# A hybrid SSM and attention layer on one core: x, four weights and B once on the SP queue, small tables on GpSimd's, a written order for ScalarE and VectorE until hT is there, W units two projections later

## The chip, the core and the metric

The kernel runs on one core of a Trainium2 chip. The metric is the device time of one execution in microseconds: 744.75 us as the median of three runs (743.58 to 747.46) for the kernel before. One further execution was taken with the hardware profiler; everything said of engines, waits and single instructions comes from it.

## What is computed

One decoder layer with float32 inputs: x is 512 tokens by 1024 channels. Cut to what matters here:

```python
h = rms_norm(x, norm_w)
u, z_s, q, k, v, z_a, r_s, r_a = split(h @ w_in)          # 1024 -> 9216
# state space branch: 64 groups of 16 channels, 64 complex states each
dt = exp(log_dt); ab = exp(lam * dt)                      # complex
bb = (ab - 1) / lam * b
h_t = ab * h_(t-1) + bb u_t ;  y_t = Re(c h_t) + d_skip * u_t
g = gelu(y); y_s = (g * sigmoid(g @ w_glu) * silu(z_s)) @ w_ssm_out
# attention branch: three dilated windows, q and k normed and rotated
y_a = (dilated_attention(rope(norm(q)), rope(norm(k)), v) * silu(z_a)) @ w_attn_out
m = sigmoid(r_s) * y_s + sigmoid(r_a) * y_a
out = x + m @ w_o
```

## The kernel before

**Number format and units of work.** Every large matmul is done in three parts (`mm3`, L108 to L110): each operand is split into a rounded part "hi" and a remainder "lo", and hi·hi, hi·lo and lo·hi are summed. A projection (`cm_unit`) takes one weight block of 1024 by 128 and all of hT (h, transposed to channels on partitions) and is 24 matmuls of 512 columns; in the attention stage there are also projections by tokens (256 columns). A weight goes through a raw buffer `w_raw` (two of them), then `w_hi` on ScalarE (L93) and `w_lo` on VectorE (L95), three buffers each. `load_w` issues the DMA on the SP queue; `get_w` hands out the next weight of a fixed plan and issues loads up to two weights ahead.

**Stages in text order.** (1) ident, x (four tiles `x_t[r]` of 128 tokens), the inverse root of the mean square for two tiles at a time (L208 to L216, called h = 0 and 1), transposes into a PSUM bank `hps` (two channel blocks a bank), and from each bank `hT_hi` (ScalarE, L227) and `hT_lo` (VectorE, L228). (2) Eight projections give u, sent to DRAM and read back in another layout (`Uj`). The first three are computed in two halves of 256 columns. Between them stand the tables of the state space branch: `exp_exact`, `sincos`, the powers `pw` (L349 to L378), their transposes `AT` and `fT`, and `BB`, `BB2` (L423 to L428, in a tile `dd`). (3) For each of eight blocks j, `w_unit(j)` forms coefficients on VectorE and GpSimd (`coef`, L252 to L254, tile `ab`), transposes them on PE (L271, bank `wps`) and copies them to W; `x_unit(j)` multiplies by Uj (L282, bank `xps`) into Xs. (4) A scan along the sequence on VectorE (L610 to L612 and its neighbours, tile `scn`), while PE does further projections ("fillers" za, zs, v, rs, ra, from the list `order`) and `kps`. (5) The y units (L731, L733) with GELU, then the glu and output projections. (6) Attention in four head pairs; the ra projections not yet done lie in the last pair's stretch between scores and values (`ptp` transposes). (7) The last projections.

**What sets the order.** The text does not fix the order on an engine. A scheduler orders the instructions by their dependences and by its own estimate of when each can start; an explicit order exists where the text asks for it. So the mask steps (L497 to L510) stand early on VectorE though they are late in the text. DMAs were issued on SP's queue, except norm_w on ScalarE's. The fillers and `n_ra` (the count of ra projections in `order`; the other ones come after the head pairs) fix which weights follow which:

```python
order = [("za", c) for c in range(NP)] + [("zs", c) for c in range(KT)] + [("v0", 0), ("v", 0)]
order += [("rs", c) for c in range(KT)] + [("ra", c) for c in range(n_ra)]
...
for j in range(3, 8):
    u_unit(j)
    wx(*((), (), (0,), (1,), (2, 3))[j - 3])
...
for js in ((4,), (5, 6), (7, 8)):
    filler()
    wx(*js)
```

`wx(j)` issues `w_unit(j)` and then `x_unit(j - 1)`. During the loading of x, the weights' first two `w_lo` were given to GpSimd (`lo_w[0] = pool`).

Of the kernel before, what the change touches and what calls it, by code (L numbers as in the profile page):

```python
# [52 lines left out]
def tile_hybrid_block(ctx: ExitStack, tc: tile.TileContext, x, positions, norm_w, w_in, lam_re, lam_im,  # L53
# [3 lines left out]
    pe, act, dve, pool, sp = nc.tensor, nc.scalar, nc.vector, nc.gpsimd, nc.sync  # L57
# [55 lines left out]
    n_ra = 2  # L113
# [48 lines left out]
    def load_w(srcs, kts, cols):  # L162
        raw = wp.tile([P, kts, cols], F32, name="w_raw", tag="w_raw", bufs=2)
        w = cols // len(srcs)
        for i, s in enumerate(srcs):
            sp.dma_start(raw[:, :, i * w:(i + 1) * w], s.rearrange("(k p) c -> p k c", p=P))
# [20 lines left out]
    dve.tensor_copy(nwc, nps[:, 0:KT])  # L187
    x_all = big.tile([P, NB, D], F32, name="x_all", tag="s3")
# [16 lines left out]
    junk = big.tile([P, D], F32, name="junk", tag="s6a")  # L205
    for h in range(2):
        for r in (2 * h, 2 * h + 1):
            act.activation(junk, x_t[r], AF.Square, accum_out=ss[:, r:r + 1])  # L208
# [3 lines left out]
        for r in (2 * h, 2 * h + 1):  # L212
            if r % 2:
                act.activation(x_t[r], x_t[r], AF.Copy, scale=rst[:, r:r + 1])
            else:
                dve.tensor_scalar(x_t[r], x_t[r], rst[:, r:r + 1], None, op0=ALU.mult)  # L216
        for q in range(KT // 2):
# [6 lines left out]
            for k in range(2):  # L224
# [4 lines left out]
                                         op0=ALU.mult, op1=ALU.subtract)  # L229
    if "hT" in dbg:  # L230
# [64 lines left out]
    lr = scr([G, N])  # L295
    li = scr([G, N])
    dt = scr([G, 1])
    sp.dma_start(lr, lam_re[0])
    sp.dma_start(li, lam_im[0])
    sp.dma_start(dt, log_dt.rearrange("o g -> g o"))  # L300
# [36 lines left out]
    dte = scr([G, 1])  # L337
    exp_exact(dte, dt, [G, 1], "ea")
    mag = scr([G, N])
    th_ = scr([G, N])  # L340
    dve.tensor_scalar(th_, lr, dte, None, op0=ALU.mult)
    exp_exact(mag, th_, [G, N], "eb")
    dve.tensor_scalar(th_, li, dte, None, op0=ALU.mult)
    sn = scr([G, N])
    cs = scr([G, N])
    sincos(sn, cs, th_, [G, N], "la")

    pw = big.tile([G, 2, 9, N], F32, name="pw", tag="s7a")
    dve.tensor_tensor(pw[:, 0, 0], mag, cs, op=ALU.mult)  # L349
    dve.tensor_tensor(pw[:, 1, 0], mag, sn, op=ALU.mult)  # L350
    den = scr([G, N])
    nr = scr([G, N])
    t1 = scr([G, N])
    t2 = scr([G, N])
    dve.tensor_tensor(den, lr, lr, op=ALU.mult)
    dve.tensor_tensor(t1, li, li, op=ALU.mult)
    dve.tensor_tensor(den, den, t1, op=ALU.add)
    dve.reciprocal(den, den)
    dve.tensor_scalar(nr, pw[:, 0, 0], -1.0, None, op0=ALU.add)
    dve.tensor_tensor(t1, nr, lr, op=ALU.mult)  # L360
    dve.tensor_tensor(t2, pw[:, 1, 0], li, op=ALU.mult)
    dve.tensor_tensor(t1, t1, t2, op=ALU.add)
    dve.tensor_tensor(pw[:, 0, 8], t1, den, op=ALU.mult)
    dve.tensor_tensor(t1, pw[:, 1, 0], lr, op=ALU.mult)
    dve.tensor_tensor(t2, nr, li, op=ALU.mult)
    dve.tensor_tensor(t1, t1, t2, op=ALU.subtract)
# [289 lines left out]
    for js in ((4,), (5, 6), (7, 8)):  # L656
        filler()
        wx(*js)
# [436 lines left out]
```

## Time and profile before

| | |
|---|---|
| median of three runs | 744.75 us (743.58 to 747.46) |
| the profiled execution | 745.33 us, of which the span of its instructions is 743.5 us |
| mean granted TensorE clock | 0.983 |
| VectorE, ScalarE, GpSimd busy | 63%, 45%, 23% of the span |
| largest groups on ScalarE and VectorE | w_hi 105.9 us (100 of 1060 ns), w_lo 124.2 us (98 of 1268 ns) |
| DMA | 85.51 MB, mean 115 GB/s |

How to read the rows: PE is the matmul engine, PEld its weight loads, DVE VectorE, ACT ScalarE, POOL GpSimd, SP the engine that issues most DMAs. A row of the timeline has the start, the duration, the engine, the line in the kernel, the operation, the tile written, the tiles read, shape, count, and in brackets how long the engine was idle before it and what released it. A row of the list of waits has who waited for whom, the total, how often, and the longest. In a row of a group the count is followed by the busy time and the mean of one in ns, then the idle time ahead of it.

### The profile page before, as it was taken

What the parts mean: (1) busy time and instruction counts of PE and PEld (TensorE: products, weight loads), DVE (VectorE), ACT (ScalarE), POOL (GpSimd) and SP (SyncE); (2) the same over time, 40 slices, a digit from 0 to 9 for tenths busy, and PEclk for the clock granted to TensorE, in tenths of its full rate; (3) what the DMA queues carried; (4) which work ended last, traced back from release to release, by engine and by line L of the source; (5) the groups of instructions that cost most, each with busy time, mean ns of one, the idle gap of its engine ahead of it and who ended that gap; (6) DMA issues with size and microseconds to landing.
All of it is one profiled execution on the core that took longest, in us unless ns stands there. A gap on an engine that the chain in (4) does not pass through costs nothing.

```text
span 743.5 us, 13321 instructions
## 1 busy us (share of the span) xinstructions
PE 702.2 (94%) x5221; PEld 615.8 (83%) x5221; DVE 468.4 (63%) x958; ACT 336.7 (45%) x628; POOL 168.7 (23%) x304
## 2 busy tenths in 40 slices
PE   3699999999979688999999999999999999999998
PEld 2687788788857477888899999899999989778997
DVE  6768757989867454674336679667747654536631
ACT  6443544233388574433143475464446435433310
POOL 3345631110001001550001224142304311200000
PEclk9899999999999899999999999999999999999999
DMA  9754654674637765447324212213211321356321
GB/s 203 129 143 110 159 114 105 144 178 118 120 101 138 136 132 143 154 133 217 91 80 120 86 57 85 59 30 98 85 46 57 95 77 57 109 179 226 124 100 57
DMA packets 156014, 85.51 MB, mean 115 GB/s; under 512 B 40232, under 2 KB 148144, under 8 KB 155824
## 3 DMA queue, kind: packets, MB, share of 16 engines
q1 hardware_dynamic: 155936, 84.66, 44.1%
q8 instruction: 41, 0.67, 0.4%
q14 instruction: 21, 0.17, 0.1%
q10 hardware_dynamic: 16, 0.00, 0.0%
HBM read 73.18 MB, written 11.47 MB: 114 GB/s over the span
## 4 chain that ended last, share of the span: by engine, by line
PE 78%; DMA 8%; DVE 6%; SPq 3%; ACT 2%; issue 2%; POOL 0%; DVEq 0%; ACTq 0%
PE pj L110 21%; PE pj L109 21%; PE pj L108 21%; DMA w_raw<-in_w_in_dram 4%; PE ot L926 3%; PE ptp L940 2%; PE sps L870 2%; PE qtp L827 1%; DMA kd<-kt 1%; DVE w_lo L95 1%; PE xps L282 1%; DMA dd<-kd 1%; PE wps L271 1%; DMA gd<-th 1%; DVE scn L610 1%
## 5 line engine op out<-in xcount | busy, mean ns | idle before, releaser
L93 ACT ACTIVATE w_hi<-w_raw 128x1024 fp32r<-128x1024 f32 x100 | 105.9, 1060 | 200.6 <-PE pj L109 89.4
L95 DVE TENSOR_TENSOR w_lo<-w_raw,w_hi 128x1024 fp32r<-128x1024 f32 x98 | 124.2, 1268 | 64.1 <-ACT w_hi L93 62.9
L108 PE MATMUL pj<-hT_hi,w_hi 128*128 128x512 f32 (+1 forms) x344 | 135.0, 395 | 9.7 <-ACT w_hi L93 5.6
L109 PE MATMUL pj<-w_lo,hT_hi 128*128 128x256 f32 x512 | 144.0, 281 | 0.0
L110 PE MATMUL pj<-w_hi,hT_lo 128*128 128x256 f32 x512 | 143.9, 281 | 0.0
L108 PE MATMUL pj<-w_hi,hT_hi 128*128 128x256 f32 x512 | 143.8, 281 | 0.0
L109 PE MATMUL pj<-hT_lo,w_hi 128*128 128x512 f32 (+1 forms) x344 | 133.5, 389 | 0.4 <-DVE hT_lo L228 0.4
L110 PE MATMUL pj<-hT_hi,w_lo 128*128 128x512 f32 (+1 forms) x344 | 133.3, 388 | 0.1
L109 PEld LDWEIGHTS pj<-w_lo,hT_hi 128*128 128x128 f32 x512 | 96.2, 188 | 1.4 <-issue 0.7
L108 PEld LDWEIGHTS pj<-w_hi,hT_hi 128*128 128x128 f32 x512 | 96.0, 188 | 1.1 <-issue 0.9
L110 PEld LDWEIGHTS pj<-w_hi,hT_lo 128*128 128x128 f32 x512 | 96.0, 188 | 0.7
L108 PEld LDWEIGHTS pj<-hT_hi,w_hi 128*128 128x128 f32 x344 | 67.0, 196 | 23.1 <-ACT w_hi L93 5.8
L110 PEld LDWEIGHTS pj<-hT_hi,w_lo 128*128 128x128 f32 x344 | 66.5, 193 | 14.5 <-issue 0.8
L109 PEld LDWEIGHTS pj<-hT_lo,w_hi 128*128 128x128 f32 x344 | 66.8, 194 | 13.5 <-DVE hT_lo L228 0.8
L814 POOL TENSOR_TENSOR rt<-qraw,tC 128x256 f32<-128x256 f32 x12 | 16.5, 1371 | 127.0 <-DVE qraw L807 93.0
L109 PE MATMUL pj<-w_lo,mT_hi 128*128 128x256 f32 x128 | 36.2, 283 | 0.0
L110 PE MATMUL pj<-w_hi,mT_lo 128*128 128x256 f32 x128 | 36.2, 283 | 0.0
L108 PE MATMUL pj<-w_hi,mT_hi 128*128 128x256 f32 x128 | 36.2, 283 | 0.0
L849 ACT ACTIVATE Pt<-Pt,st 128x256 f32<-128x256 f32 (+1 forms) x64 | 31.0, 487 | 5.0 <-DVE st L847 4.8
L799 DVE TENSOR_REDUCE ssq<-qsq 128x8 f32<-128x512 f32 x24 | 16.4, 685 | 26.3 <-ACT qsq L798 26.2
L835 ACT ACTIVATE qkp<-qtp,wcol 128x512 fp32r<-128x512 f32 (+1 forms) x32 | 20.7, 685 | 20.7 <-PE qtp L827 15.6
L796 ACT COPY qraw<-pj 128x512 f32<-128x512 f32 x24 | 14.1, 586 | 35.0 <-PE pj L110 34.8
(272 smaller groups left out, 1368.5 us busy)
## 6 DMA issues: line engine op xcount, KB each, us to landing
w_raw<-in_w_in_dram SPq DMA_DIRECT2D x40, 512.0 KB
w_raw<-in_w_in_dram SPq DMA_DIRECT2D x64, 256.0 KB
dd<-kd SPq DMA_DIRECT2D x8, 512.0 KB
w_raw<-in_w_glu_dram SPq DMA_DIRECT2D x8, 512.0 KB
w_raw<-in_w_ssm_out_dram SPq DMA_DIRECT2D x8, 512.0 KB
w_raw<-in_w_o_dram SPq DMA_DIRECT2D x8, 512.0 KB
x_all<-in_x_dram SPq DMA_DIRECT2D x4, 512.0 KB
ud<-uT SPq DMA_DIRECT2D x8, 256.0 KB
```

The source lines that it names most:

```text
L93: act.activation(hi, src, AF.Copy, scale=scale)
L95: e.tensor_tensor(lo, src, hi.bitcast(F32), op=ALU.subtract)
L108: pe.matmul(o, lh, rh, start=first, stop=False, skip_group_check=True)
L109: pe.matmul(o, lh, rl, start=False, stop=False, skip_group_check=True)
L110: pe.matmul(o, ll, rh, start=False, stop=last, skip_group_check=True)
L799: dve.tensor_reduce(sq[:, 2 * b:2 * b + 2], s.rearrange("p (r h d) -> p r h d", r=2, h=4), AX.X, ALU.add)
L814: pool.tensor_tensor(t1, rh[:, :, :, 0:16], cv.broadcast_to([P, NB * 2, 2, 16]), op=ALU.mult)
L835: act.activation(hi, ps[sl], AF.Copy, scale=w)
L849: act.activation(o, o, AF.Exp, bias=nm, scale=-1.0, accum_out=st[:, kind, 1, h, b:b + 1])
L870: pe.matmul(pss[h][:, cols], QT[x_][po, 0, cb], KA[y_][po, ks], start=n == 0, stop=n == 2, skip_group_check=True)
L926: pe.matmul(o, v, pts[h][:, (2 * i + k) * P:(2 * i + k + 1) * P], start=first, stop=kind == 1 and b == NB - 1 and k == 1, skip_group_check ...
L940: pe.transpose(ps[:, (2 * i + k) * P:(2 * i + k + 1) * P], Pt[:, h, kind, 2 * bb + i, k * P:(k + 1) * P], ident)
```

## The change

(a) x, the first four weights and B are put on the SP queue first, in that order and each after the one before. The four weights go to a tile of their own, `w_early`, and are not in line for the two raw buffers. (b) B is read from DRAM once (`D1`); its swapped copy `D2` is made by two copies from SBUF to SBUF, issued on GpSimd's queue. (c) lam_re, lam_im, log_dt, positions and the q and k norm weights are issued on GpSimd's queue instead of SP's. (d) Until hT is complete, every instruction of ScalarE and VectorE that the text issues there is bound to the text's order (`Traced`, `in_order`); the sum of squares is done half on ScalarE and half on VectorE; `w_lo` is on VectorE throughout. Table work is bound to come after the second half's x has been scaled (`issue_after(normed...)`). (e) W units begin after the eighth u projection and are spread over five fillers, two projections later than before; `n_ra` goes from 2 to 4, so that four instead of two ra projections lie in `order`.

```diff
-    pe, act, dve, pool, sp = nc.tensor, nc.scalar, nc.vector, nc.gpsimd, nc.sync
+    pe, pool, sp = nc.tensor, nc.gpsimd, nc.sync
+    in_order = [False]
+    class Traced:
...
+            def call(*a, **k):
+                r = f(*a, **k)
+                if in_order[0] and name != "dma_start":
+                    if self.last is not None:
+                        tc.add_manual_dep(r.ins, self.last.ins.name, NOSYNC, reason="in order")
+                    self.last = r
+                return r
...
+    act, dve = Traced(nc.scalar), Traced(nc.vector)
...
-    n_ra = 2
+    n_ra = 4
...
     def load_w(srcs, kts, cols):
...
+        if len(loaded) < len(early):
+            raw = early[len(loaded)]
+        else:
...
+    pool.dma_start(lr, lam_re[0])
+    pool.dma_start(li, lam_im[0])
+    pool.dma_start(dt, log_dt.rearrange("o g -> g o"))
...
-    lo_w[0] = pool
-    for r in range(NB):
-        sp.dma_start(x_t[r], xv[r])
-        if r in (1, 2):
-            prefetch(len(loaded) + 1)
-    lo_w[0] = dve
+    early_t = big.tile([P, 4, KT, P], F32, name="w_early", tag="s2")
+    early = [early_t[:, i] for i in range(4)]
...
+    moves = [(x_t[r], xv[r]) for r in range(NB)]
+    moves += [(early[i], plan[i][0][0].rearrange("(k p) c -> p k c", p=P)) for i in range(4)]
+    moves += [(D1[0:64], b_re[0].rearrange("g n q -> n g q")), (D1[64:128], b_im[0].rearrange("g n q -> n g q"))]
+    prev = None
+    for o, i in moves:
+        if prev is None:
+            prev = sp.dma_start(o, i)
+        else:
+            with tc.issue_after(prev.ins):
+                n = sp.dma_start(o, i)
+            prev = n
+    pool.dma_start(D2[64:128], D1[0:64])
+    pool.dma_start(D2[0:64], D1[64:128])
...
+    def sum_sq(r):
+        if r % 2 == 0:
+            act.activation(junk[:, 0], x_t[r], AF.Square, accum_out=ss[:, r:r + 1])
+        else:
+            dve.tensor_tensor_reduce(junk[:, 1], x_t[r], x_t[r], 1.0, 0.0, ALU.mult, ALU.add, ss[:, r:r + 1])
+    def scale_x(h):
...
+        dve.tensor_scalar(x_t[2 * h], x_t[2 * h], rst[:, 2 * h:2 * h + 1], None, op0=ALU.mult)
+        act.activation(x_t[2 * h + 1], x_t[2 * h + 1], AF.Copy, scale=rst[:, 2 * h + 1:2 * h + 2])
+    def turn_x(h):
...
+    in_order[0] = True
+    for r in range(3):
+        sum_sq(r)
+    scale_x(0)
+    sum_sq(3)
+    prefetch(1)
+    turn_x(0)
+    prefetch(2)
+    scale_x(1)
+    normed = dve.last
+    prefetch(3)
+    turn_x(1)
+    in_order[0] = False
+    normed = normed, act.last
...
+    with tc.issue_after(normed[0].ins), tc.issue_after(normed[1].ins):
+        dte = scr([G, 1])
+        exp_exact(dte, dt, [G, 1], "ea")
...
-    sp.dma_start(D1[0:64], bv[0])
-    sp.dma_start(D1[64:128], bv[1])
-    sp.dma_start(D2[0:64], bv[1])
-    sp.dma_start(D2[64:128], bv[0])
...
     for j in range(3, 8):
         u_unit(j)
-        wx(*((), (), (0,), (1,), (2, 3))[j - 3])
+    wx(0)
...
-    sp.dma_start(pos_i, positions[0].rearrange("(i r) -> i r", r=NB))
+    pool.dma_start(pos_i, positions[0].rearrange("(i r) -> i r", r=NB))
...
-    for js in ((4,), (5, 6), (7, 8)):
+    for js in ((1,), (2, 3), (4,), (5, 6), (7, 8)):
         filler()
         wx(*js)
```

Because every call of ScalarE and VectorE now goes through the wrapper, their instructions in the changed kernel all carry the wrapper's line, L73.

**Where it moves instructions.** On ScalarE, for the first half of x, before. `junk` is the square of an x tile, `hps` with a number is one PSUM bank of transposes:

```order
L93 ACTIVATE w_hi_105<-w_raw_103 128x1024
L208 ACTIVATE junk_112,scr_81<-x_all_93 128x1024
L227 ACTIVATE hT_hi_110<-hps_129,nwc_89 128x256
L227 ACTIVATE hT_hi_110<-hps_138,nwc_89 128x256
L227 ACTIVATE hT_hi_110<-hps_147,nwc_89 128x256
L227 ACTIVATE hT_hi_110<-hps_129,nwc_89 128x256
L227 ACTIVATE hT_hi_110<-hps_156,nwc_89 128x256
L227 ACTIVATE hT_hi_110<-hps_138,nwc_89 128x256
L227 ACTIVATE hT_hi_110<-hps_147,nwc_89 128x256
L227 ACTIVATE hT_hi_110<-hps_156,nwc_89 128x256
```

And ScalarE in the same place of the changed kernel:

```order
L73 ACTIVATE x_all_96<-x_all_96,scr_81 128x1024
L73 ACTIVATE w_hi_132<-w_early_97 128x1024
L73 ACTIVATE hT_hi_111<-hps_136,nwc_89 128x256 x2
L73 ACTIVATE hT_hi_111<-hps_145,nwc_89 128x256 x2
L73 ACTIVATE hT_hi_111<-hps_154,nwc_89 128x256 x2
L73 ACTIVATE hT_hi_111<-hps_163,nwc_89 128x256 x2
L73 ACTIVATE w_hi_172<-w_early_97 128x1024
```

The second weight's `w_hi` and a square have left the place ahead of the first `hT_hi`, and the banks, of which three were opened before the first one's second `hT_hi`, are now done one after the other, both halves of a bank in a row.

On GpSimd, at the start, before. `ident` is the unit matrix that the transposes need, and the first IOTA makes the column numbers from which the masks start:

```order
masks.py:197 MEMSET ident_82 128x128
L382 MEMSET AT_471 128x64
L383 MEMSET AT_471 128x64
L430 MEMSET sgn_539 64x1
masks.py:199 ISA
masks.py:199 AFFINE_SELECT ident_82<-ident_82 128x128
L431 MEMSET sgn_539 64x1
L494 IOTA scr_81 128x128
```

And GpSimd there in the changed kernel:

```order
masks.py:197 MEMSET ident_82 128x128
L219 DMA scr_81<-in_lam_re_dram 64x64
L220 DMA scr_81<-in_lam_im_dram 64x64
L221 DMA scr_81<-in_log_dt_dram 64x1
masks.py:199 ISA
masks.py:199 AFFINE_SELECT ident_82<-ident_82 128x128
L442 MEMSET AT_473 128x64
L443 MEMSET AT_473 128x64
L483 MEMSET sgn_536 64x1
L484 MEMSET sgn_536 64x1
L535 DMA scr_81<-in_positions_dram 128x4
L548 IOTA scr_81 128x128
```

Three DMA issues now stand between the two steps of `ident`, and a fourth ahead of the IOTA.

On VectorE, from the last coefficients of W to the first step of the scan (`scn<-Xs`), before. `sza` is a silu step of a za projection, `p12` belongs to the y stage:

```order
L252 TENSOR_TENSOR ab_532<-dd_526,AT_471 128x1024
L95 TENSOR_TENSOR w_lo_1111<-w_raw_1108,w_hi_1110 128x1024
L454 SCALAR_TENSOR_TENSOR sza_839<-th_1031,pj_1006 128x512
L254 TENSOR_TENSOR ab_532<-ab_532 128x1024
L529 COPY wcol_878<-wcp_879 128x6
L95 TENSOR_TENSOR w_lo_1303<-w_raw_1300,w_hi_1302 128x1024
L454 SCALAR_TENSOR_TENSOR sza_839<-th_1139,pj_1114 128x512
L680 TENSOR_SCALAR p12_1214<-cps_1211,sgn_539 128x128
L252 TENSOR_TENSOR ab_532<-p12_1214,AT_471 128x576 x2
L610 TENSOR_TENSOR scn_928<-Xs_218,scn_928 128x1024
```

And VectorE from the last coefficients of W in the changed kernel, where `z` is a silu step of a zs projection, the filler that follows za:

```order
L73 TENSOR_TENSOR ab_529<-dd_98,AT_473 128x1024
L73 TENSOR_TENSOR ab_529<-ab_529 128x1024
L73 TENSOR_TENSOR w_lo_1370<-w_raw_1367,w_hi_1369 128x1024
L73 SCALAR_TENSOR_TENSOR z_1204<-th_1205,pj_1179 128x512
L73 TENSOR_TENSOR w_lo_1426<-w_raw_1423,w_hi_1425 128x1024
L73 SCALAR_TENSOR_TENSOR z_1398<-th_1399,pj_1373 128x512
L73 TENSOR_SCALAR p12_1281<-cps_1278,sgn_536 128x128
L73 TENSOR_TENSOR ab_529<-p12_1281,AT_473 128x576 x2
L73 TENSOR_TENSOR scn_814<-Xs_231,scn_814 128x1024
```

The fillers whose silu steps lie next to the scan's first step are zs instead of za: two more projections, with their weights, lie ahead of the scan than before.

More of the change, by code (lines that the diff above doesn't have):

```diff
@@ L204, in tile_hybrid_block @@
     rb_ = scr([P, NB])
[L205 to L208, printed above, removed]
+    junk = big.tile([P, 2, D], F32, name="junk", tag="s6b")
+    def sum_sq(r):
[4 more added lines that the diff above has]
+    def scale_x(h):
         w = slice(2 * h, 2 * h + 2)
@@ L335, in sincos @@
         dve.tensor_scalar(cs, cs, 1.0, None, op0=ALU.add)
[L337 to L362, printed above, removed]
```

141 lines of the change are left out of this document (83 added, 58 removed).

## The prediction, made without the time of the changed kernel

> **What bounds the kernel now.** I read the page's busy shares first, then the busy time by stretches, since a share of 94% is a mean over stages that differ.
>
> ```profile
> PE 702.2 (94%) x5221; PEld 615.8 (83%) x5221; DVE 468.4 (63%) x958; ACT 336.7 (45%) x628; POOL 168.7 (23%) x304
> sum 300.00, PE 262.22; mean PE 4.37
> sum 440.00, PE 439.93; mean PE 20.00
> 25.00:30.00 5.00, 0.51 (x5) 0.89 0.88 200
> 30.00:35.00 5.00, 3.81 (x16) 0.50 0.54 153
> 245.00:250.00 5.00, 4.50 (x11) 0.50 0.50 91
> ```
>
> The two sums are PE's busy time in stretches of 0 to 300 us and of 300 to 740 us. In the row of one stretch stand its length, PE's busy time and instructions, the granted clock, the DMA share and GB/s. From 300 us on PE never waits, so the change can win or lose only ahead of 300, where PE is idle for 37.8 us. Idle time has an echo, too: after the empty stretch from 25 to 30 the clock was 0.50, and again in 245 to 250. Next comes the list of what PE waited for (total, times, longest).
>
> ```profile
> PE hps L223 <- DVE x_all L216: 9.5, 1, 9.5
> PE pj L108 <- ACT w_hi L93: 5.6, 1, 5.6
> PE pj L108 <- ACT th L469: 4.1, 1, 4.1
> PE wps L271 <- DVE ab L254: 2.8, 2, 2.1
> ```
>
> The first, second and fourth lie where the change acts: x normalised too late, the third weight too late, the coefficients of W too late. The third lies behind the scan. The timelines of PE and VectorE, and VectorE's own waits from 119 to 206 us, show how tight the scan is:
>
> ```profile
> 117.06 0.44 PE L677 MATMUL cps<-ident,cn 128*128 128x128 f32 x2
> 119.27 1.22 DVE L610 TENSOR_TENSOR scn<-Xs,scn 128x1024 f32<-128x1024 f32 x1
> 204.89 0.69 DVE L612 TENSOR_TENSOR Xs<-Xs,scn 128x512 f32<-128x512 f32 x1
> 207.33 0.34 PE L733 MATMUL yps<-ab,uss 128*64 128x64 f32 x4 [2.10 <-ACT uss L721]
> DVE w_lo L95 <- ACT w_hi L93: 5.6, 4, 2.3
> ```
>
> The scan starts 2.2 us after PE has done the last X unit (117.06) and runs until 205.6, 86.3 us, in which VectorE waits 5.6 us; 1.8 us after it PE begins the y matmuls, having waited 2.1. So two chains are nearly level here: PE's own projections, and start, W, X, scan, y. The second one ends last.
>
> **The first projections.** Before:
>
> ```profile
> 7.54 0.17 DVE L210 TENSOR_SCALAR scr<-scr 128x2 f32<-128x2 f32 x1 [3.61 <-ACT junk L208]
> 9.61 2.34 POOL L95 TENSOR_TENSOR w_lo<-w_raw,w_hi 128x1024 fp32r<-128x1024 f32 x1 [7.48 <-ACT w_hi L93]
> 9.72 2.25 DVE L105 SCALAR_TENSOR_TENSOR scr<-scr 128x2 f32<-128x2 f32 x1
> 12.01 0.75 DVE L216 TENSOR_SCALAR x_all<-x_all,scr 128x1024 f32<-128x1024 f32 x1
> 15.24 1.33 ACT L227 ACTIVATE hT_hi<-hps,nwc 128x256 fp32r<-128x256 f32 x3
> 16.75 0.47 DVE L228 SCALAR_TENSOR_TENSOR hT_lo<-hps,nwc,hT_hi 128x256 fp32r<-128x256 f32 x1
> 17.25 1.57 ACT L227 ACTIVATE hT_hi<-hps,nwc 128x256 fp32r<-128x256 f32 x4 [0.68 <-DVE hT_lo L228]
> 20.11 0.47 DVE L228 SCALAR_TENSOR_TENSOR hT_lo<-hps,nwc,hT_hi 128x256 fp32r<-128x256 f32 x1
> 1.97 0.29 DVE L497 CUSTOM_DVE_ANT_0 scr<-scr,ident 128x128 f32<-128x128 f32 x1 [1.97 <-POOL scr L494]
> 3.63 0.29 DVE L510 TENSOR_TENSOR maskB<-maskB 128x128 f32<-128x128 f32 x1
> 24.57 5.37 DMA w_raw<-in_w_in_dram
> L95 DVE TENSOR_TENSOR w_lo<-w_raw,w_hi 128x1024 fp32r<-128x1024 f32 x98 | 124.2, 1268 | 64.1 <-ACT w_hi L93 62.9
> 44.59 1.20 PE L388 MATMUL atp<-ident,pw 64*64 64x64 f32 x32
> ```
>
> Three things act on the first half of x. A 2-wide step that takes 0.17 us took 2.25 beside GpSimd's w_lo; that stall goes, since every w_lo is now VectorE's. But the mask steps, which filled 1.97 to 3.92 while VectorE had nothing else, now stand between the sum of squares and the inverse root, and cost about the same 1.95 us again. So the inverse root comes at some 11.4 instead of 12.0. ScalarE's first hT_hi no longer stands behind the second weight and a square, and comes at 14.5 instead of 15.24; VectorE has the first weight's w_lo (1.27 us) ahead of hT_lo, which starts at 15.0.
>
> Then the text's order costs. The second hT_hi of a bank waits for the first hT_lo of that bank (the 0.68 us in the row at 17.25). Before, ScalarE went through three banks first, and the eight hT_lo took from 16.75 to 20.6, 3.8 us. Now each bank goes hi, lo, hi, lo by turns. Only the next bank's first hi runs beside the last lo, so a bank costs three steps of 0.44 to 0.47 us and the hand-overs, 1.5 us, and four cost 6.0: the last hT_lo ends at 21.0. The second half follows: w_lo to 22.9, inverse root to 25.3 (12 steps like that at 7.54, a little over 2 us), x scaled 26.4, transposes 28.0, the third weight's w_lo to 29.6 after some 19 small table steps; then eight hT_lo with 30 small steps of 0.15 to 0.2 us among them, to 38.2.
>
> What is won is the weight: it landed 5.37 us after its late issue, PE stood still for it and then ran at 0.50. By the rows of the next part a matmul of the first projections takes 0.117 us (half of 0.233, being half as wide). Of their 144, 48 need only the first half and two weights, and two more need no w_lo; so 94 are left at 29.6, and only the last eleven hang on the last hT_lo. They end at 40.6, or 42.2 if the first of them run at half clock; I take 41.3, against 44.5. But the tables finish later as well: pw at about 41.6, and the fourth weight's w_lo, which stands behind it on VectorE, at 43.4. PE waits there for 2 us.
>
> **The W and X stretch.** PE's rates there, and how long a projection takes:
>
> ```profile
> 109.99 1.20 PE L282 MATMUL xps<-Uj,W 128*64 128x64 f32 x32
> 111.12 1.09 PE L271 MATMUL wps<-ident,ab 128*128 128x128 f32 x8
> 112.15 1.20 PE L282 MATMUL xps<-Uj,W 128*64 128x64 f32 x32
> 641.53 0.58 ACT L477 ACTIVATE th<-pj 128x512 f32<-128x512 f32 x1
> 647.13 0.58 ACT L477 ACTIVATE th<-pj 128x512 f32<-128x512 f32 x1
> 53.59 1.21 DVE L423 TENSOR_TENSOR dd<-dd,fT 128x1024 f32<-128x1024 f32 x1
> 71.16 1.09 PE L271 MATMUL wps<-ident,ab 128*128 128x128 f32 x8 [0.78 <-DVE ab L254]
> 105.78 0.68 DVE L454 SCALAR_TENSOR_TENSOR sza<-th,pj 128x512 f32<-128x512 f32 x1
> ```
>
> From start to start an X unit is 1.13 us, a W unit 1.03, and a projection of 24 matmuls 5.60, 0.233 each. After 43.4, five whole projections (28.0) and the table matmuls (1.2 in the row at 44.59, 1.5 with the small ones) bring the first W to 73.0, against 71.16 with 22 fewer projection matmuls done. Its coefficients need 17.5 us from the first step of BB on VectorE (53.59 to 71.1 before); BB comes at about 55.2 now (32 of those matmuls, 7.5, stand ahead of the last transpose it needs; then 0.7 for the transposes, some 2.4 for ScalarE's copies and 1.27 for a w_lo), so they are there at 72.7. Both waits of this stretch, 2.8 us, go; the cover is 0.3 us thin for the first, and should VectorE be later, PE waits as much. Between the first W and the last X stand 8 W units (8.2), 8 X (9.0), the small matmuls (1.7) and 154 projection matmuls (35.9; before there were 97): 54.8 us, to 127.8 instead of 117.06. The scan starts at 130.0 instead of 119.27, **10.8 us later**.
>
> **The scan and the rest.** VectorE's steps between the first and last scan step are the same, 14 w_lo among them, but three silu steps now come ahead of it (0.6 us each, a little under the 0.68 of the row at 105.78, since neighbours overlap). That gives 84.5 us, and y starts at 216.3, 9.0 later. Two projections (11.2 us) that stood in the last head pair's cover are done by then, so the gain at this point is 2.2 us. PE itself gets to the y matmuls at about 208 and waits 8 us for the scan instead of 2.1. Such a pause slows the clock after it: in the row of 245 to 250, 4.5 us ran at half clock, 2.2 us lost. Shorter pauses stood here before, too, so I add a third of that, 0.7, between nothing and 2.2. The y stretch has the same seven projections in both and the same chain through DRAM; I take no difference, with bounds of -3 and +3 (its wait of 4.1 us could nearly go, or most of another such wait could come).
>
> At the end only two of the later ra projections are left between scores and values instead of four:
>
> ```profile
> 644.15 0.62 DVE L903 TENSOR_SCALAR Pt<-Pt,sfb 128x256 f32<-128x256 f32 x2
> 651.75 1.47 PE L940 MATMUL ptp<-ident,Pt 128*128 128x128 f32 x12
> ```
>
> The last Pt is ready at 644.8, seven us before PE asks for it. With 32 matmuls fewer (7.5 us) PE asks at 644.3, and first for the half that is older. I take 0.5 us, bounds 0 and 2.
>
> GpSimd's DMAs are the one price that the trace lacks: no transfer is issued there before. Three stand ahead of ident's last step, and a fourth ahead of the iota that the masks need. The nearest rows are SP's issues:
>
> ```profile
> 24.02 0.43 SPq L518 DMA_DIRECT2D scr<-in_k_norm_w_dram  x1
> 16.92 2.78 SPq L414 DMA_DIRECT2D dd<-in_b_re_dram  x1
> ```
>
> With p for each, the iota comes at 2.2 + 4p and the masks want it at 7.6, so p is free up to 1.35. I take the small tables' row, 0.43, as the nearest: nothing. The other end is 2.78, and 5.7 us. The Trainium skill ("SBUF — State Buffer", Who interferes with whom) speaks against this move: DMAs issued on GpSimd need it to write descriptors, and while VectorE runs a two-port operation it can't. The same page has a transfer of 620 ns that took 3100 so; as an estimate from that page, 3.1 us for p would make the sum 7.0 us worse. The row at 9.72 agrees in that the two engines shut each other out, though there GpSimd was the one that held; no run here shows the descriptors.
>
> **Sum.** At the y matmuls: 10.8 later for the scan's start, less 1.8 for its length, less 11.2 for the projections done, -2.2. The clock gives +0.7, the end +0.5: **-1.0 us**. The profiled run took 745.33 (span 743.5 and 1.8 around it), so the forecast is 744.3; the median of the runs shown is 744.75, 0.6 lower.
>
> **Rivals.** *The scan shrinks.* VectorE's 5.6 us of waits in it are for w_hi, of weights that come through two raw buffers. If PE, being ahead with other work, frees buffers sooner and those waits go, the run takes 738.7. For it: four waits of up to 2.3 us, just at late weights. Against it: a weight is late by its transfer (5.37 us for one at 24.57), and the transfers stay.
>
> *GpSimd's issues are dear.* The price decides. At p = 2.5 ident and iota come 4.6 us late, every us reaches the scan since nothing between slackens, and 748.9 is over the bound; at 2.78 the run takes 750.0. For it: SP's row of 2.78. Against it: that row's transfer has thousands of short pieces, and these tables have 64 to 128.
>
> *The turns of a bank overlap after all*, so that the order by text costs nothing: then hT is there 2.2 us earlier in each half, and the run takes 739.9. The row at 17.25 speaks against it.
>
> *The change doesn't do what it says*: VectorE is still behind with the coefficients, both W waits stay, and the run takes 744.3 + 2.8 = 747.1, no change that can be measured.
>
> **Numbers.** A measurement of this kernel can tell about 0.5% (3.7 us) from no change. Within that, 741.0 to 748.5, lie the forecast and the last rival: 0.47. The shrinking scan and the overlapping turns, or a better y stretch with either in part: 0.28. Dear issues or a worse y stretch on top of a late W: 0.25. The range takes in the ends of the rivals and of the y bounds: 736 to 752.
>
> **What would show it.** The first half's hT_lo come by turns at 0.5 and 1.0 us and end near 21; there is no wait for the third weight; PE's first three projections are over near 41; no W wait; the first scan step stands at 130 and the y matmuls at 216 after a wait of some 8 us. If the first transpose of x comes later than 13 us, or the masks end after 10, the dear issues hold; if the scan takes under 80 us, the first rival. If PE waits for coefficients again, my count for VectorE from 43 to 73 is wrong.

## The result and the profile after

The changed kernel takes 750.82 us (median of six runs, 748.35 to 751.29), the kernel before 745.19 (743.58 to 747.46) on the same chip: a ratio of 1.0068, 95% interval 1.0048 to 1.0088. It is slower by 0.7%, where 0.1% faster was forecast. The profiled execution took 751.29 us with a span of 749.5; before, the span was 743.5. So 6.0 us have to be found.

The busy shares and the list of PE's waits from 0 to 300 us, changed kernel:

```profile
PE 704.7 (94%) x5221; PEld 615.8 (82%) x5221; DVE 475.9 (63%) x964; ACT 334.8 (45%) x624; POOL 172.6 (23%) x310
PE hps L273 <- DVE x_all L73: 7.8, 1, 7.8
PE yps L786 <- issue: 6.6, 1, 6.6
PE yps L788 <- ACT uss L73: 6.2, 1, 6.2
PE pj L133 <- ACT th L73: 5.7, 4, 2.6
PE vtp L623 <- ACT vt L73: 5.4, 1, 5.4
```

The wait for the third weight (5.6 us) and those for W's coefficients (2.8) are gone, and PE's wait for x is shorter. In their place stand a longer wait for the scan (`uss`, 6.2 instead of 2.1) and a new one ahead of `vtp`, the transpose of v. Two more lie behind the scan: 5.7 us for `th` (4.1 before), and 6.6 us at a y matmul (L786) that reads M, the matrix that comes back through `kd` in DRAM. The profile names no releaser for this last one; the wait at the same place of the kernel before is 2.6. From the timelines of PE and VectorE, the places that answer to those shown of before (`cps` follows PE's last X unit):

```profile
20.62 0.48 DVE L73 SCALAR_TENSOR_TENSOR hT_lo<-hps,nwc,hT_hi 128x256 fp32r<-128x256 f32 x1 [0.54 <-ACT hT_hi L73]
42.53 0.52 PE L448 MATMUL atp<-ident,pw 64*64 64x64 f32 x8 [2.83 <-DVE pw L73]
44.15 0.50 PE L135 MATMUL pj<-hT_hi,w_lo 128*128 128x512 f32 x1 [0.45 <-DVE w_lo L73]
45.00:50.00 5.00, 5.00 (x16) 3.93 (x15) 5.00 (x14) 1.32 (x2) 4.35 (x7) 0.68 0.69 181
76.56 1.03 PE L336 MATMUL wps<-ident,ab 128*128 128x128 f32 x8
132.43 0.44 PE L732 MATMUL cps<-ident,cn 128*128 128x128 f32 x2
134.64 1.22 DVE L73 TENSOR_TENSOR scn<-Xs,scn 128x1024 f32<-128x1024 f32 x1
223.74 1.42 DVE L73 TENSOR_TENSOR Xs<-Xs,scn 128x512 f32<-128x512 f32 x2
226.67 0.48 PE L788 MATMUL yps<-ab,uss 128*64 128x64 f32 x4 [6.22 <-ACT uss L73]
```

The last hT_lo of the first half ends at 21.1, and PE is done with the first three projections at 39.7 (before 44.7). But there it stops: it has no work until the tables' `pw` (2.83 us) and the fourth weight (0.45), and runs the stretch from 45 to 50 at a clock of 0.68. The first W comes at 76.6, 5.4 later than before, the last X unit ends 15.4 later, the scan takes 90.5 us (134.64 to 225.16) instead of 86.3, and the y matmuls start 19.3 later. Two projections (11.2 us) are done by then that used to come at the end, so the net loss is 8.1 us. The stretch behind gives back 2.5: from the y matmuls to the first matmul of the projection by w_ssm_out it takes 126.2 us instead of 128.7.

```profile
352.86 0.39 PE L133 MATMUL pj<-yT_hi,w_hi 128*128 128x512 f32 x1
336.07 0.39 PE L108 MATMUL pj<-yT_hi,w_hi 128*128 128x512 f32 x1
```

(the first row of the changed kernel, the second of before). What comes after it costs 0.4 more than the 11.2 us explain: 8.1 - 2.5 + 0.4 = 6.0, the difference of the spans.

### The profile page after: what moved, and what is told of

Its sections match the earlier page's. It is cut to its first block, busy times and chain, and to the rows that moved or that the text cites. A ratio compares the mean times of both kernels' runs of the same rounds, so it can differ in the third digit from the quotient of the medians.

```text
span 749.5 us, 13338 instructions
## 1 busy us (share of the span) xinstructions
PE 704.7 (94%) x5221; PEld 615.8 (82%) x5221; DVE 475.9 (63%) x964; ACT 334.8 (45%) x624; POOL 172.6 (23%) x310
## 4 chain that ended last, share of the span: by engine, by line
PE 76%; DVE 6%; DMA 6%; ACT 4%; issue 3%; POOL 2%; SPq 0%; DVEq 0%; ACTq 0%; POOLq 0%
PE pj L134 21%; PE pj L133 21%; PE pj L135 21%; PE ot L981 3%; ACT uss L73 2%; PE ptp L995 2%; PE sps L925 2%; PE qtp L882 1%; DMA w_early<-in_w_in_dram 1%; DMA w_raw<-in_w_in_dram 1%; DVE scr L73 1%; PE xps L347 1%; DMA gd<-th 1%; DMA Uj<-ud 1%; DVE ab L73 1%
## 5 line engine op out<-in xcount | busy, mean ns | idle before, releaser
L73 ACT ACTIVATE w_hi<-w_raw 128x1024 fp32r<-128x1024 f32 x96 | 101.7, 1060 | 194.8 <-PE pj L134 93.7
L73 DVE TENSOR_TENSOR w_lo<-w_raw,w_hi 128x1024 fp32r<-128x1024 f32 x96 | 121.4, 1266 | 73.8 <-ACT w_hi L73 72.9
L73 ACT ACTIVATE Pt<-Pt,st 128x256 f32<-128x256 f32 (+1 forms) x64 | 31.0, 487 | 4.9 <-DVE st L73 4.8
L73 DVE TENSOR_REDUCE ssq<-qsq 128x8 f32<-128x512 f32 x24 | 16.3, 684 | 26.1 <-ACT qsq L73 25.9
L73 DVE TENSOR_TENSOR ab<-p,AT 128x576 f32<-128x576 f32 x32 | 24.2, 780 | 12.1 <-ACT p L73 8.5
L73 ACT ACTIVATE qkp<-qtp,wcol 128x512 fp32r<-128x512 f32 (+1 forms) x32 | 20.7, 685 | 20.7 <-PE qtp L882 15.6
```

The source lines that it names most:

```text
L73: r = f(*a, **k)
```

## The experiments

The runs stand in the order in which they were made: four, four, three, one. All times are ratios to the kernel before on the same chip. The places are those of the one profiled execution of each kernel: e7's took 748.9 us, the longest of its ten, and e11's 749.5, the shortest of its four; the others lie within 1.8 us of their median. "Net" is the start of the y matmuls against 207.3 of before, less 11.2 us where two more projections are done by then; "behind" is the time from there to the projection by w_ssm_out.

| run | ratio, 95% interval | first W | last X ends | scan takes | y matmuls | net | behind |
|---|---|---|---|---|---|---|---|
| before | 1 | 71.2 | 117.1 | 86.3 | 207.3 | 0 | 128.7 |
| changed | 1.0068 (1.0048 to 1.0088) | 76.6 | 132.5 | 90.5 | 226.7 | +8.1 | 126.2 |
| e1 front only | 0.9958 (0.9937 to 0.9978) | 72.8 | 117.7 | 85.7 | 207.3 | 0.0 | 126.3 |
| e2 late W only | 1.0055 (1.0029 to 1.0081) | 75.9 | 131.6 | 91.8 | 227.1 | +8.6 | 123.9 |
| e3 kt on GpSimd's queue | 0.9998 (0.9978 to 1.0017) | 76.3 | 132.5 | 84.9 | 221.2 | +2.7 | 126.6 |
| e4 fourth weight first | 1.0086 (1.0064 to 1.0108) | 78.9 | 134.3 | 92.3 | 230.3 | +11.8 | 123.7 |
| e5 e1, tables first | 1.0053 (1.0033 to 1.0073) | 74.2 | 124.4 | 84.2 | 212.7 | +5.4 | 128.2 |
| e6 e1, two banks | 1.0070 (1.0046 to 1.0094) | 69.2 | 121.7 | 84.3 | 210.0 | +2.6 | 132.0 |
| e7 e1, kt on GpSimd's | 0.9981 (0.9953 to 1.0010) | 72.1 | 118.5 | 87.8 | 210.2 | +2.8 | 129.4 |
| e8 e5, e6 and e7 | 1.0074 (1.0042 to 1.0105) | 68.9 | 120.7 | 83.7 | 209.0 | +1.7 | 133.1 |
| e9 e1, fillers behind W | 1.0143 (1.0118 to 1.0169) | 72.6 | 114.6 | 91.9 | 210.5 | +3.2 | 136.3 |
| e10 before, fillers behind W | 1.0095 (1.0073 to 1.0116) | 70.8 | 113.6 | 90.5 | 207.9 | +0.6 | 134.8 |
| e11 e9, kt on GpSimd's | 1.0118 (1.0094 to 1.0143) | 72.7 | 114.5 | 86.7 | 206.0 | -1.3 | 134.3 |
| e12 cn by four loads | 1.0049 (1.0028 to 1.0071) | 75.6 | 131.5 | 88.2 | 223.6 | +5.0 | 128.0 |

### The two halves of the change (e1, e2)

e1 is the changed kernel with W where it was:

```diff
-    n_ra = 4
+    n_ra = 2
...
         u_unit(j)
-    wx(0)
+        wx(*((), (), (0,), (1,), (2, 3))[j - 3])
...
-    for js in ((1,), (2, 3), (4,), (5, 6), (7, 8)):
+    for js in ((4,), (5, 6), (7, 8)):
```

> The changed kernel with the W units and n_ra = 2 put back as they were before; the loading order, the tables on GpSimd's queue and the written order stay. Theory A (two causes: in the changed kernel the scan begins late because everything behind the third projection is late, and it is longer because a weight's DMA waits on the SP queue behind the store of kt): the tables are as late as in the changed kernel, so W's coefficients come at 72.5 and 77.5 us and PE waits for both again; the last X unit ends near 118.5 (117.06 before, 132.43 changed), the scan takes 86 us as before and the y matmuls start near 209. The run takes 746 to 748 us. Theory B (the later W units alone cost the time, the new start is a gain): the run takes 742 us or less, with the last X unit before 115.

e2 is the kernel before with the same lines the other way round.

> The kernel before with nothing but the later W units and n_ra = 4. Theory A: PE does 22 more projection matmuls ahead of the first W (5.1 us) and 57 more up to the last X (13.3), less the two waits for coefficients of 2.8 us, so the last X unit ends near 131; if the scan takes its 86 us the y matmuls start near 220 and, after 11.2 us of projections won back, the run takes 746 to 747; if the weight is held up in the scan as in the changed kernel (4 to 6 us), 750 to 752. Theory B: 750 or more without any hold-up in the scan.

PE's rows of e1 (first three) and of VectorE and PE in e2 (last three):

```profile
72.82 1.09 PE L336 MATMUL wps<-ident,ab 128*128 128x128 f32 x8 [0.75 <-DVE ab L73]
77.80 0.44 PE L336 MATMUL wps<-ident,ab 128*128 128x128 f32 x2 [2.25 <-DVE ab L73]
207.29 0.34 PE L788 MATMUL yps<-ab,uss 128*64 128x64 f32 x4 [1.46 <-ACT uss L73]
180.62 1.23 DVE L95 TENSOR_TENSOR w_lo<-w_raw,w_hi 128x1024 fp32r<-128x1024 f32 x1 [6.55 <-ACT w_hi L93]
181.11 1.11 PE L568 MATMUL vtp<-ident,vt 128*128 128x128 f32 x4 [5.85 <-ACT vt L563]
227.12 0.48 PE L733 MATMUL yps<-ab,uss 128*64 128x64 f32 x4 [6.22 <-ACT uss L721]
```

In e1 the places of theory A come true (coefficients at 72.8 and 77.8 after waits of 0.75 and 2.25 us, last X at 117.7), and the y matmuls start as before, at 207.29: the 4.6 us that the first three projections won are gone by the first W, since the tables are no earlier. The time did not come true: 742.34 us, 0.4% faster than before, where A said 746 to 748. What is won is won behind the y matmuls (126.3 instead of 128.7). That is close to the time of theory B (742 or less), but not its reason.

e2 has the whole loss at the y matmuls (+8.6) without anything of the new start, and the hold-up too: VectorE waits 6.55 us for w_hi and PE 5.85 ahead of vtp. So the later W units bring both the late scan and the hold-up in it. The last X unit ends where theory A put it (131.6 for 131); the run, 749.4 us, lies a little under the 750 to 752 of A with the hold-up.

### What holds the weight up (e3, e12)

The queue of SP, GpSimd, ScalarE and PE in the changed kernel, around the long wait:

```profile
160.84 1.27 SPq L517 DMA_DIRECT2D gd<-z  x1
167.11 0.62 SPq L759 DMA_DIRECT2D kd<-kt  x1
169.59 0.60 SPq L762 DMA_DIRECT2D dd<-kd  x1
170.28 1.46 SPq L194 DMA_DIRECT2D w_raw<-in_w_in_dram  x1
165.43 0.53 POOL L729 COPY cn<-cn 128x64 f32<-128x64 f32 x1 [10.82 <-DMA cn<-in_c_re_dram]
165.90 0.77 POOL L728 COPY cn<-cn 128x64 f32<-128x64 f32 x1
166.63 0.46 POOL L758 TENSOR_TENSOR kt<-kt,dg 16x128 f32<-16x128 f32 x1
179.92 1.06 ACT L73 ACTIVATE w_hi<-w_raw 128x1024 fp32r<-128x1024 f32 x1 [11.88 <-DMA w_raw<-in_w_in_dram]
181.50 1.11 PE L623 MATMUL vtp<-ident,vt 128*128 128x128 f32 x4 [5.38 <-ACT vt L73]
```

They are read backwards. PE waits for vt, which stands on ScalarE behind w_hi; w_hi waits for its weight, which was issued only at 170.28, because SP had stood from 162.1 to 167.1 before the store of kt; that waited for GpSimd's addition to kt (166.63), which stood behind two copies of cn, and they for a load of cn. Nothing in that chain needs the weight, and the weight needs nothing of it: they share queues. The load of M (`dd<-kd`, 512 KB like the weight) went out 0.7 us ahead of the weight on the same queue, and the weight took 9.6 us from its issue to its w_hi. VectorE waits for the same w_hi, 6.2 us in the middle of the scan.

e3 takes kt's store and M's load off SP:

```diff
-        sp.dma_start(kd[j, :, :, 0:128], kt.rearrange("q g k p -> q g (k p)"))
+        pool.dma_start(kd[j, :, :, 0:128], kt.rearrange("q g k p -> q g (k p)"))
...
-        sp.dma_start(M.rearrange("p (g k) -> p g k", g=8),
+        pool.dma_start(M.rearrange("p (g k) -> p g k", g=8),
```

> The changed kernel with the store of kt to kd and the load of M from kd issued on GpSimd's queue instead of SP's. Theory A: no weight waits behind kt any more, VectorE's wait of 6.2 us for w_hi in the scan and PE's wait of 5.4 us ahead of vtp go, the scan takes 84 to 86 us instead of 90.5, and the run takes 745 to 747 us. Rival C (the weight is late by its raw buffer and its transfer, whatever queue kt is on): the wait for w_hi stays over 4 us, and the run takes 749 to 752.

VectorE's waits for w_hi in the scan (total, times, longest), of the changed kernel, of e3, and of e12:

```profile
DVE w_lo L73 <- ACT w_hi L73: 11.4, 5, 6.2
DVE w_lo L73 <- ACT w_hi L73: 6.4, 6, 2.4
DVE w_lo L73 <- ACT w_hi L73: 10.3, 4, 3.2
```

PE's order up to there is the changed kernel's, the last X unit ends at the same 132.5, and the scan takes 84.9 us instead of 90.5. PE's wait ahead of vtp is gone, and the run is back at the time of before (744.5 us). Theory A's waits and times hold, but its way there, the late issue behind kt, is the smaller part of it. In e3, the addition to kt on GpSimd, SP behind it, and the same weight on ScalarE:

```profile
167.54 0.45 POOL L758 TENSOR_TENSOR kt<-kt,dg 16x128 f32<-16x128 f32 x1
168.02 0.33 SPq L743 DMA_DIRECT2D dg<-in_d_skip_dram  x1
168.44 0.38 SPq L194 DMA_DIRECT2D w_raw<-in_w_in_dram  x1
172.96 1.06 ACT L73 ACTIVATE w_hi<-w_raw 128x1024 fp32r<-128x1024 f32 x1 [4.91 <-DMA w_raw<-in_w_in_dram]
```

In e3 SP stands even longer for that addition, 8.7 us instead of 4.9, since the load of dg (L743), which stayed on SP, waits for it as well. The weight behind it goes out at 168.44, only 1.85 us earlier. But M's load is no longer ahead of it (GpSimd issues it at 172.1), and the weight is there after 4.5 us instead of 9.6: of the 7.0 us by which its w_hi is earlier, 5.1 are the faster transfer. So e3 does not show what kt's store alone costs; it moved M's load too, and that is the larger part. Rival C is wrong on the wait and the time, but right that the transfer counts.

e12 goes one link further back: the swapped half of cn is loaded instead of copied, and kt stays on SP.

```diff
-        pool.tensor_copy(cn[:, 1, 0:64], cn[:, 0, 64:128])
-        pool.tensor_copy(cn[:, 1, 64:128], cn[:, 0, 0:64])
+        sp.dma_start(cn[:, 1, 0:64], c_im[0].rearrange("g p n -> (g p) n")[rows])
+        sp.dma_start(cn[:, 1, 64:128], c_re[0].rearrange("g p n -> (g p) n")[rows])
```

> The changed kernel with the swapped half of cn loaded from DRAM (four loads on SP's queue instead of two), so that GpSimd makes no copy that waits for a load ahead of its addition to kt; kt's store stays on SP's queue, and PE's order is the changed kernel's. Theory A (the hold-up in the scan is a chain: load of cn, GpSimd's copies behind it, the addition to kt behind these, kt's store behind that on SP, the weight's load behind that): the store goes out near 162.5 instead of 167.1 us, the weight's load near 166 instead of 170.3, VectorE's wait of 6.2 us shrinks to 1 to 2, the scan takes 85 to 87 us and the run 745 to 748. Rival H (kt's store is held by its own addition or by the load of dg, not by cn): the wait stays over 4 us, 750 to 752.

```profile
160.63 0.45 POOL L758 TENSOR_TENSOR kt<-kt,dg 16x128 f32<-16x128 f32 x1 [7.00 <-ACT kt L73]
162.28 0.62 SPq L759 DMA_DIRECT2D kd<-kt  x1
166.03 0.93 SPq L194 DMA_DIRECT2D w_raw<-in_w_in_dram  x1
176.67 1.23 DVE L73 TENSOR_TENSOR w_lo<-w_raw,w_hi 128x1024 fp32r<-128x1024 f32 x1 [3.23 <-ACT w_hi L73]
```

The links are where theory A put them (store at 162.28, weight's load at 166.03), so cn is the first of the chain. The size is half: M's load still stands 0.7 us ahead of the weight, the weight still takes 9.5 us, to 175.6, and VectorE waits 3.2 for it; another weight is late by 3.1 near the scan's end. The scan takes 88.2 us and the run 749.6, above the 745 to 748 expected. Both the late issue and the slow transfer behind M's load make the wait: e12, whose scan starts 1.0 us earlier, brings the issue 3.3 us forward against the scan, and e3 shortens the transfer by 5.1. No run moves M's load alone.

### The start (e4 to e8)

e4 puts the fourth weight's split ahead of the tables in the changed kernel (`prefetch(4)` behind `turn_x(1)`).

> The changed kernel with the fourth weight's w_hi and w_lo put into the written order right behind the last hT_lo, ahead of the table steps. Theory A: PE goes on with the fourth projection at 39.8 instead of 44.2 us and does not run at a lower clock after it (1.6 us), the tables finish some 1.5 us later; the first W then waits for its coefficients at about 74 (76.56 changed), the scan starts 2 to 3 us earlier, and the run takes 748 to 749. Rival D (the chain through the tables is the one that counts, and it gets longer): the first W not before 76, and the run 750.5 to 752.

Theory A missed, rival D is right. ScalarE in e4, then PE:

```profile
38.69 1.06 ACT L73 ACTIVATE w_hi<-w_early 128x1024 fp32r<-128x1024 f32 x1 [1.17 <-PE pj L134]
39.77 1.28 ACT L73 ACT_TABLE_LOAD   x1
41.23 1.02 ACT L73 COPY uT<-pj 128x512 f32<-128x512 f32 x1
78.93 1.09 PE L337 MATMUL wps<-ident,ab 128*128 128x128 f32 x8 [0.66 <-DVE ab L73]
```

The fourth w_hi itself waits until PE lets go of a weight buffer (38.7), then ScalarE loads its table for the sine, and only then copies out a result (`uT<-pj`), of the kind that holds a PSUM buffer PE needs; PE goes on at 42.3, when this copy and the sine step beside it are over. The first W waits for coefficients at 78.9, 2.4 later than in the changed kernel.

The next runs stand on e1. e5 holds the splits of the sixth to eighth weight back behind `pw`, e6 forms hT from two banks at a time, e7 is e1 with e3's edit, and e8 has all three. Their cores, in this order (e7's diff is e3's):

```diff
+            if pw_end[0] is not None and len(loaded) < 8:
+                after_pw.enter_context(tc.issue_after(pw_end[0].ins))
             split(hi, lo, raw, lo_eng=lo_w[0])
...
-        for q in range(KT // 2):
-            ps = bank("hps")
+        for q0 in range(0, KT // 2, 2):
+            pair = [bank("hps") for _ in range(2)]
...
+            for k in range(2):
+                for i, ps in enumerate(pair):
...
+                    act.activation(hT_hi[:, kk, t], ps[:, 256 * k:256 * k + 256], AF.Copy, scale=nwc[:, kk:kk + 1])
+                for i, ps in enumerate(pair):
...
+                    dve.scalar_tensor_tensor(hT_lo[:, kk, t], ps[:, 256 * k:256 * k + 256], nwc[:, kk:kk + 1],
```

> The kernel of e1 with the sixth, seventh and eighth weight's split (w_hi and w_lo) put behind the last step of pw. Theory A (in e1 the new start wins nothing at the y matmuls because the tables bound the first W units): BB comes 2 to 4 us earlier, PE's two waits for coefficients (0.75 and 2.25 us in e1) go, the last X unit ends at 113 to 115.5 (117.7 in e1), the scan starts 2 to 4 us earlier, and the run takes 739 to 741. Rival E (VectorE is the bound as a whole up to the scan, so its order does not matter): PE waits for the later w_lo instead, the last X unit stays at 117 to 118, and the run takes 742 to 744.

> The kernel of e1 with hT formed from two banks at a time (hi of both, lo of both, hi of both, lo of both) instead of one. Theory A: without the turns in one bank the last hT_lo of the first half ends at 19 instead of 21, and the first three projections end at 36 to 38 instead of 40.1; as the tables bound what follows, they gain as far as VectorE has its hT_lo out of the way, 1 to 2 us, and the run takes 740.5 to 741.5. Rival F (the turns cost nothing, or the start does not matter at all): the last hT_lo of the first half stays at 21, or the run at 742 to 743.

> The kernel of e1 with the store of kt and the load of M on GpSimd's queue, as in e3. In e1 no weight of the scan is held up by kt, so theory A expects no change up to the y matmuls (207.3) and at most 1 to 2 us of the waits in the y stretch: 740.5 to 742.5. If kt's place on SP's queue costs something everywhere (rival C turned round), the scan shortens by 2 us or more and the run takes 738 to 740.

> The kernel of e1 with the edits of e5, e6 and e7 together. Theory A: the last X unit ends at 111 to 114, the y matmuls start at 201 to 204, PE having waited for the scan, and the run takes 736 to 740. Rival E: the last X unit stays past 116, and the run takes 741 or more.

PE behind the last X unit in e5 and in e6, and e6's first y matmuls:

```profile
124.36 0.44 PE L736 MATMUL cps<-ident,cn 128*128 128x128 f32 x2
121.59 0.44 PE L736 MATMUL cps<-ident,cn 128*128 128x128 f32 x2
209.97 0.48 PE L792 MATMUL yps<-ab,uss 128*64 128x64 f32 x4 [6.02 <-ACT uss L73]
```

e6 has the start that theory A expected: the last hT_lo of the first half ends at 18.6 (21.1 with one bank at a time, so the turns do cost 2.5 us), the first three projections end at 37.5 (40.1 in e1) and the first W comes at 69.2. Yet in e5, e6 and e8 the last X unit ends later than in e1, not earlier, and all three are slower than before, which neither theory of e5 and e6 had said (e8's rival E had both). For the late X the cause is one for all: the scheduler put 220 instead of 195 projection matmuls between the first three projections and the last X, a whole projection more (25 by 0.233 us is 5.8). The scan is 1.4 to 2.0 us shorter than e1's, PE waits 6.0 for it, and the y matmuls start 1.7 to 5.4 us later. It is the change's own step, in small and without having been asked for. But only e5's loss against e1 lies mostly there. In e6 and e8 the larger part lies behind the y matmuls, where the same work takes 132.0 and 133.1 us instead of e1's 126.3; in e6 PE waits 3.1 and 7.5 us there for loads of M. So these runs leave open what an earlier start alone would bring. e7 hardly moved the last X but lengthened the scan by 2.1 in its profiled execution (waits for w_hi of 7.6 in all, 5.5 in e1). Its time, 744.3 us, is above the 740.5 to 742.5 expected and can't be told from before.

### The other way (e9 to e11)

If projections ahead of the last X cost, fewer should win. e9 takes the three fillers between the W units of e1 to the scan (thirteen there instead of ten); e10 does it to the kernel before, with one filler left, which gives PE nearly the same order; e11 is e9 with e3's edit and with one filler left, and PE's order up to the y matmuls is e9's.

```diff
-    for js in ((4,), (5, 6), (7, 8)):
-        filler()
+    for i, js in enumerate(((4,), (5, 6), (7, 8))):
+        if i < 0:
+            filler()
         wx(*js)
...
-    n_scan = 10
+    n_scan = 13
```

> The kernel of e1 with the three fillers that stood between the W units moved behind them (thirteen fillers in the scan instead of ten): 87 instead of 99 projection matmuls between the first W and the last X, the other way from the change. Theory A (start, W, X, scan, y is the chain that ends last, so a matmul less ahead of the last X is worth its time at the scan's start, until PE is the one that arrives last): the last X unit ends 2 to 3 us earlier (115, 117.7 in e1), the scan starts that much earlier and has half a w_lo more in it, the y matmuls start near 205 (207.3), where PE no longer waits, and the run takes 740 to 742. Rival G (it does not matter where the projections stand, only how long PE is idle in all): y matmuls at 207 to 208 and 742 to 744.

> The kernel before with the same edit but for one filler, which gives PE the same order up to the scan: 83 instead of 97 matmuls between the first W and the last X. Theory A: the last X unit at 114 (117.1), the y matmuls at 204 to 206 (207.3), the run 742 to 744, if the weights of the scan are not held up by kt, and 745 to 748 if they are. Rival G: no change of the y matmuls, 744 to 746.

> The kernel of e9 (with one filler left between the W units, which gives the same order on PE) with the store of kt and the load of M on GpSimd's queue. If in e9 a weight of the scan is held up behind kt as in the changed kernel, theory A expects the scan 4 to 6 us shorter than in e9; if none is, 740 to 744, no better than e9.

VectorE's waits for w_hi in the scan and the first y matmuls, e9 and then e11:

```profile
DVE w_lo L73 <- ACT w_hi L73: 9.1, 3, 4.5
210.48 0.34 PE L789 MATMUL yps<-ab,uss 128*64 128x64 f32 x4 [1.03 <-ACT uss L73]
DVE w_lo L73 <- ACT w_hi L73: 2.6, 6, 0.5
206.03 0.34 PE L789 MATMUL yps<-ab,uss 128*64 128x64 f32 x4 [0.65 <-ACT uss L73]
```

The last X unit ends 3.1 us earlier in e9, as expected. But weights are held up again (waits of 9.1 us; the two long ones, 4.4 and 4.5, are for weights whose load went out 0.7 us behind M's and took 9.8 and 9.5), the scan takes 91.9, and the y matmuls start 3.2 later. With kt off SP's queue (e11) the waits are 2.6, the scan 86.7, and the y matmuls start at 206.0, 1.3 earlier than in e1: a second pair that shows the hold-up, worth 5.3 us of the scan here. All three (e10 too) are nevertheless among the slowest of the study, because the stretch behind takes 134 to 136 us. Theory A is right here on the last X and, without the hold-up, on the y matmuls, and wrong on the times; rival G is wrong as well: equal work in another place is 1% slower.

## Why the prediction was wrong

**First half of x, first three projections: right.** 21.1 for 21.0, 39.7 for 41.3, the fourth at 44.15 for 43.4. GpSimd's issues took 0.54 to 0.76 us each, under the 1.35 up to which they are free, so they cost the nothing that was taken. The longest:

```profile
1.31 0.76 POOL L219 DMA_DIRECT2D scr<-in_lam_re_dram  x1 [0.36 <-issue]
```

ident is there at 3.5, long before x, so that rival is out. By the Trainium skill ("SBUF — State Buffer", Who interferes with whom) they could have starved beside VectorE; no row here shows it, and VectorE had little to do in those first 6 us.

**The first W: mis-sized by 3.6 us** (73.0 forecast, 76.6). Three terms are short and make 3.3 of it. The fourth projection came 0.75 later. PE had stood for 3.3 us in two pieces from 39.7 on and then ran the five us of 45 to 50 at 0.68 of its clock, 1.6 us, an echo that the prediction reckoned with behind the scan and forgot here. The tables' transposes took 2.4 instead of 1.5 (four pieces). The coefficients were there in time, as forecast. (The Trainium skill, "TensorE: Matmul & The Clock Gate", What's actually happening, gives about 3.4 us without work as what halves the clock; here 2.83 and 0.45 us with work between them were enough for a loss.)

**W to X: nearly right.** From the first W to the last X 55.9 us for 54.8. The scan starts at 134.64 for 130.0.

**The scan's length: the step that failed.** "VectorE's steps between the first and last scan step are the same ... That gives 84.5 us." The steps were, and with kt and M on another queue the scan takes 84.9 (e3). It took 90.5: VectorE's waits for w_hi in it grew from 5.6 to 11.4 us, which the prediction had left at 5.6. It counted the steps on VectorE and left out SP's queue, on which the later W units change what stands ahead of which weight; of that queue it had a rival with the other sign (the 5.6 us of waits going), none with this one. e2 shows that the hold-up belongs to the later W units, e3 and e11 that it hangs on kt's store and M's load being on SP's queue. Two things make it up: the weight goes out late, with a load of cn at the head of the chain (e12 gives 2.3 us of the scan back), and it then takes 9.6 us behind M's load instead of 4.5 without it (e3). Neither is new as such: in the kernel before, SP stands 4.5 us for an addition to kt, and a weight 0.7 us behind M's load takes 9.4:

```profile
138.08 0.62 SPq L707 DMA_DIRECT2D dd<-kd  x1
138.80 1.00 SPq L166 DMA_DIRECT2D w_raw<-in_w_in_dram  x1
148.25 1.06 ACT L93 ACTIVATE w_hi<-w_raw 128x1024 fp32r<-128x1024 f32 x1 [4.98 <-DMA w_raw<-in_w_in_dram]
```

VectorE waits only 1.4 us there. In the changed kernel both fall on one weight, for which VectorE stands from 174.8 to 181.0.

**The projections won back: right in size** (11.2), and too little. Without the hold-up the net at the y matmuls would be +2.7 (e3) instead of the -2.2 forecast; the difference is for the most part the first W's 3.6 and the 1.1 up to the last X.

**PE's wait for the scan: near (6.2 for 8), in part by luck.** PE itself came to the y matmuls at 220.5 instead of 208, late by the first W and by the same weight (5.4 us ahead of vtp), so both ends of the wait had slipped by 10 to 12 us. Without the hold-up it is 7.8 (e3). The end is right (0.4 for 0.5).

**The y stretch: forecast 0 with bounds of 3, measured -2.5 with the clock.** Over all runs it goes from 123.7 to 136.3 us at equal work, so it could not be left at zero with bounds of 3. In e1 it is the whole gain. Before, a wait of 4.1 us for th and its echo stood there; in e1 two waits for th of 2.4 together do. In the changed kernel its waits for th are longer than before (5.7) and so is the one at M (6.6); what went are mainly the waits for coefficients (2.3 and 3.5 us before). Why they fall as they do was not settled: no run changed this stretch alone.

In sum: +4.6 for the scan's start, +6.0 for its length, -0.3 for the step from there to the y matmuls, -3.2 for what lies behind (-2.5 where +0.7 was forecast) and -0.1 at the end make 7.0 us more than forecast: 751.3, which is the profiled execution's time.

## What to carry to other kernels

When a block of work is moved later, list what it passes on the DMA-issuing queue, not only on the engines: a store that waits for a slow helper holds up every load behind it, behind a large load the next one took twice as long here, and the engine that suffers has nothing to do with either. An engine that gets ahead wins nothing where another chain (here the tables) ends later, and its pause costs clock on top; look which one ends last before paying for the lead. And try the parts one by one: here one half of the change is faster than before by 0.4% (e1), and only the other half made the whole slower.

## What the runs showed of the hardware

A weight of 512 KB, which took 5.4 us from issue to use at 24.6 us before the change, took 9.6 at 170.3 and 9.5 in e12, with M's load of 512 KB issued 0.7 us ahead of it on the same queue. Over all runs, the sixteen weights of the scan stretch that were waited for and stood 0.7 to 1.2 us behind M's load on SP took 9.4 to 10.0 us. That z's stores are issued right behind does not do it: they are in e3, too, where the weight took 4.5. A step of VectorE with two operands of 1024 elements takes 1.21 to 1.26 us alone and 2.95 beside GpSimd's (VectorE, then GpSimd, changed kernel):

```profile
59.83 2.95 DVE L73 TENSOR_TENSOR dd<-dd,ab 128x1024 f32<-128x1024 f32 x1 [1.83 <-POOL ab L475]
59.76 1.93 POOL L478 TENSOR_TENSOR ab<-dd,fT 128x1024 f32<-128x1024 f32 x1
```

VectorE's step ends 1.1 us after GpSimd's, about its own time later. The 2-wide step of 2.25 us before the change likewise lasts until GpSimd's step is over, so it looks like the same shutting-out in another place: taking w_lo from GpSimd removed one such meeting, others remained.
